# Recurrent mixer: two of four convolution channel groups as 64x64 diagonal products on the array's quarters, and the inversion's small products in turn over the quarters

## Chip, cores and metric

The kernel runs on 1 core of one Trainium2 chip. The metric is the device time of one execution in microseconds (us), the median of several runs.

## What is computed

A trunk of 256 tokens by 1024 features: feed-forward, mixer, feed-forward in each of two layers, with RMS norms around every part. The change is in the first layer's mixer, which has two halves with 512 channels each, a recurrence over 8 heads of 64 and a causal convolution over 31 tokens for each channel by itself:

```python
def mixer_ab(h, ...):
    proj = h @ w_in
    ...
    y = rwkv7_scan(rh, hs(decay), kh, vh, kk, hs(a))
    ...
    y_a = ((y + bonus.reshape(b, t, D_RWKV)) * g.astype(f32)).astype(h.dtype)
    c_val, c_gate = split_cols(proj[..., COLS_RWKV:], [D_CONV, D_CONV])
    glu = c_val * jax.nn.sigmoid(c_gate)
    conv = lax.conv_general_dilated(
        glu, conv_w[:, None, :], window_strides=(1,), padding=[(CONV_WIDTH - 1, 0)],
        dimension_numbers=('NWC', 'WIO', 'NWC'), feature_group_count=D_CONV) + conv_b
    y_b = jax.nn.silu(layer_norm(conv, conv_ln_g, conv_ln_b, CONV_LN_EPS))
    return jnp.concatenate([y_a, y_b], axis=-1) @ w_out
```

The reference runs the recurrence token by token; the kernel runs it in four chunks of 64 tokens, with the inverse of a unit triangular 64x64 matrix for each chunk and head.

## The kernel before

The stages of the program are feed-forward 0, the recurrent mixer (`mixer_a`), feed-forwards 1 and 3, the attention mixer and feed-forward 4. The mixer treated here lies at about 200 to 402 us. Its parts are given out in the order of the table `ORDER`; a scheduler then sets the order on each engine, and every engine works through its own list in order. Products with float32 operands show as two records each in the trace.

The parts that matter, in the order of the program:

- `qmats` and `amats`: products of 64 rows of the chunks, into banks named `acc00` to `acc11`, which `abank` gives out in turn. VectorE evicts those of `amats` (names `ak`, `ar`, lines 816 and 819) with masks.
- `glu`: the input projection of the convolution, gated. It comes in two halves of two channel groups each: `z` (line 843) from PSUM on VectorE, its sigmoid on ScalarE (844), `glu` on VectorE (845).
- `invert`: the blocks of 16 on VectorE, over DRAM; then `doubling`: ten calls of `each`, 16 products of 64x64x64 each, `acc<-T,Q`, `acc<-G,WT`, `acc<-WT,G` (line 585 is the helper that records every small product). The numbers #1 to #10 below are these calls. In `each` all eight heads of one column half come first, then those of the other.
- `bonus`: on GpSimd (POOL), `Wg` and `gg`, lines 884 to 887; `wlo` on line 99 is the lower part of a weight page, some of which POOL makes.
- `conv`: 31 taps (shifts by d tokens) for each of four groups of 128 channels. VectorE has groups 0 and 1 (`feed`, line 924, 60 taps). Group 3 is scaled on ScalarE into `cz` (912) and added on POOL (913). Group 2 is split: 24 taps on TensorE (`pfeed`), each a product with a 128x128 matrix `dw` that holds the tap's weights on its diagonal and is made on ScalarE from the identity (904); the other taps on ScalarE and POOL in a sum of their own. `feed` and `pfeed` say how many taps go behind which instruction.
- `convend` and `conv_norm`: the sums added (961), then transposes (936), statistics, transposes back (949), and the two parts of the output for the projection.
- `state`: for each of four chunks `vz,ak` and `ur` products into `py`, its copy `R` (ScalarE, 982), `pz` = `acc<-R,G`, `vz` (VectorE, 986), `pn` = `acc<-vz,kb`, `SB` (996), `py` again (`gu<-vz,ar`), and at the end of a tile of 128 tokens a norm and transposes (1015).
- `outproj` (370): 96 products of 128x128x512, first those with the convolution's half; then feed-forward 1 begins (223).

Of the kernel before, what the change touches and what calls it, by code (L numbers as in the profile page):

```python
# [39 lines left out]
def label(key):  # L40
    """The kind of a key of weights."""
    if key[0] in "gd":
        return f"{key[0]}{key[2]}" if key[2] < 2 else key[0]
    return "".join(str(z) for z in key)


class Stream:
    """Weights in the order of their use: raw tiles of [128, 1024], and their two parts in pages of float32r."""
# [6 lines left out]
    def add(self, key, ap, cols):  # L55
        """ap: [128, n * 1024] of DRAM; the pages are seen as [128, 1024 // cols, cols]."""
# [36 lines left out]
class Kernel:  # L93
# [21 lines left out]
    def post(self, t, acc, gpost, half, eps, last=False):  # L115
        """x[t] += half * rms_norm(acc) * gpost, the sums in PSUM; eps: of half ** -2 times the mean square."""
# [33 lines left out]
    def pre(self, t, j):  # L150
        """x[t] transposed, times the norm's gains, in two parts; and rstd."""
# [3 lines left out]
        for h in range(2):  # L155
# [3 lines left out]
            for k in range(4):  # L159
                kk = 4 * h + k  # L160
                g = self.gain(j, kk)
                nc.scalar.activation(self.xth[:, kk, ts], ps[:, k * P:(k + 1) * P], AF.Copy, scale=g)  # L162
                nc.vector.scalar_tensor_tensor(out=self.xl(kk)[:, ts], in0=ps[:, k * P:(k + 1) * P], scalar=g,  # L163
                                               in1=self.xth[:, kk, ts].bitcast(F32), op0=ALU.mult, op1=ALU.subtract)
# [11 lines left out]
    def xl_tile(self, h):  # L176
        return self.c.tile([P, 4, 256], F32R, name=f"xl{h}")

# [15 lines left out]
    def units(self):  # L194
        """The parts of a layer's work: ("t", b, t), a block of 256 columns for 128 tokens, or ("c", b, h), 128 columns for all."""
# [7 lines left out]
    def ffn(self, j, rstd, nxt, then):  # L203
        """x += 0.5 * rms_norm(swiglu(rms_norm(x))); then: keys of weights to prepare near the end.
        The factor rstd of the products with w_up is left to the norm behind."""
# [7 lines left out]
        def gu(u):  # L213
            W.upto(self.gkey(j, u))
            G = W.get(self.gkey(j, u))
            if u[0] == "t":
                ps = self.bank("gu", 2)
                n = 0
                for k in range(8):
                    hi, lo = G[k // 2]  # L220
                    xh, xl = (z[:, u[2] * P:(u[2] + 1) * P] for z in (self.xth[:, k, :], self.xl(k)))
# [102 lines left out]
    def abank(self):  # L324
        self.turn = (self.turn + 1) % 4
        return self.bank(("acc00", "acc01", "acc10", "acc11")[self.turn])

    def xunit(self, key, t, late=False):
        """x[t] times a block of 512 columns: [128 tokens, 512] in PSUM; late: not ahead of the latest transposes of x."""
# [3 lines left out]
        for k in range(8):  # L333
            hi, lo = G[k // 2]
            xh, xl = (z[:, t * P:(t + 1) * P] for z in (self.xth[:, k, :], self.xl(k)))
# [6 lines left out]
    def wunit(self, key, groups):  # L342
        """Groups of 128 columns of a block, transposed: [128 columns, group, 256 tokens] in PSUM."""
        ps = self.bank("gu", 2)
        G = self.w.get(key)
        for j, g in enumerate(groups):
            n = 0
            for k in range(8):
                hi, lo = (z[:, k, :] for z in G[g])
                xh, xl = self.xth[:, k, :], self.xl(k)  # L350
# [5 lines left out]
    def outproj(self, j, key, y, nxt, behind=None):  # L356
        """x += rms_norm(y @ w); y(k, t): the two parts of a [128, 128] block of y transposed."""
# [19 lines left out]
    def across(self, rstd):  # L377
        """rstd of the tokens along the free dim, on all partitions: [128, 256]."""
# [10 lines left out]
    def mixer_c(self, j, rstd, nxt, then):  # L389
# [43 lines left out]
        def forget():  # L433
            ps = self.bank("tr", 2)[0:16, 0:256]
            n = 0
            for k in range(8):
                for l, r in ((fhi, self.xth[:, k, :]), (flo, self.xth[:, k, :]), (fhi, self.xl(k))):
# [63 lines left out]
        def values(c, g):  # L501
# [10 lines left out]
            hi, lo = (z[:, g, :] for z in y0) if c == 0 else (self.xth[:, 4 + g, :], self.xl(4 + g))  # L512
# [45 lines left out]
        def y(k, t):  # L558
            ts = slice(t * P, (t + 1) * P)
            return tuple(z[:, ts] for z in ([z[:, k, :] for z in y0] if k < 4 else (self.xth[:, k, :], self.xl(k))))  # L560
# [3 lines left out]
    def mixer_a(self, j, rstd, nxt, then):  # L564
# [9 lines left out]
        # pages of two groups, [2 groups, 2 tiles, 4 * 64]: for both chunks of a tile what pairs with Z (b or u) and what pairs  # L574
        # with V (k or r), on the sides where the state has them
# [6 lines left out]
        m = {}  # L582

# [46 lines left out]
        def shifted(dst, ps, mu, i0):  # L630
            """Token shift of two groups of columns: (1 - mu) * p + mu * p_prev."""
# [7 lines left out]
        def lora():  # L639
# [6 lines left out]
            for dst, b, bias in ((sg, 0, "db"), (ic, 64, "ib")):  # L646
                for h in range(2):
                    ps = self.abank()
# [547 lines left out]
```

## Time and profile before

| what | value |
|---|---|
| median of 3 runs | 1130.53 us (1130.3 to 1131.13) |
| profiled execution, first to last instruction | 1130.1 us |
| TensorE (PE) busy | 1076.5 us, 95% |
| VectorE (DVE) | 669.1 us, 59% |
| ScalarE (ACT) | 568.3 us, 50% |
| GpSimd (POOL) | 256.1 us, 23% |
| mean granted clock of TensorE | 0.981 |
| mixer, the stretch from 300 to 402.5 us | see the rows below |

The profile gives the span of its execution and no other time for it; the median of the runs is 0.4 us above that span. Times in rows count from the start of the span. A row of the timeline merges equal instructions: start, length, engine, line, operation, what is written and read, shapes, their number, and in brackets how long the engine was idle just before and who ended that. For products the shape is rows * columns of the array and then partitions x elements of what is moved.

### The profile page before, as it was taken

To read this page: it belongs to the slowest core of one execution; us is meant where nothing else is said; L and a number is where in the kernel's file an instruction comes from. 1 tells how busy PE (TensorE), PEld (TensorE's weight loads), DVE (VectorE), ACT (ScalarE), POOL (GpSimd) and SP (SyncE) were. 2 spreads that over 40 slices of the span, in tenths; PEclk is the share of its full clock that TensorE was granted. 3 is DMA by queue.
4 is the path that set the end of the run, shared out by engine and by line. 5 is a ranking of instruction groups with operands and counts; after the bars stand their busy time and mean duration, and the time that the engine had idled before them with its cause. 6 is when DMAs were issued, how large, how long until landed. Compare 5 with 4: busy or idle time off the path is not lost.

```text
span 1130.1 us, 17646 instructions
## 1 busy us (share of the span) xinstructions
PE 1076.5 (95%) x6955; PEld 947.5 (84%) x6955; DVE 669.1 (59%) x1064; ACT 568.3 (50%) x933; POOL 256.1 (23%) x194
## 2 busy tenths in 40 slices
PE   7999999978788899999989999999999989999997
PEld 5899988867777789999878999988887768999986
DVE  4465662389888547556535555836667655555722
ACT  7444553554364365345455444635666845444611
POOL 4200006282744051000070000000564541000000
PEclk9999999989988999999999999999999999999999
DMA  9766785154601146557654465744273562665400
GB/s 352 253 209 187 229 305 177 50 166 115 169 2 38 32 174 206 204 187 270 213 176 126 150 244 179 240 157 132 93 284 109 189 202 95 223 189 185 150 1 37
DMA packets 65261, 189.27 MB, mean 167 GB/s; under 512 B 18300, under 2 KB 19612, under 8 KB 65178
## 3 DMA queue, kind: packets, MB, share of 16 engines
q1 hardware_dynamic: 55674, 186.70, 49.2%
q10 hardware_dynamic: 9504, 1.44, 0.7%
q8 instruction: 54, 0.88, 0.3%
q14 instruction: 29, 0.24, 0.1%
HBM read 184.68 MB, written 2.92 MB: 166 GB/s over the span
## 4 chain that ended last, share of the span: by engine, by line
PE 82%; DVE 8%; DMA 3%; ACT 2%; issue 2%; POOL 2%; SPq 0%; POOLq 0%; ACTq 0%; DVEq 0%
PE gu L352 30%; PE acc L263 21%; PE gu L223 15%; PE gu L338 5%; PE acc L370 3%; PE acc L585 2%; PE gu L585 2%; DVE cv L924 2%; DVE wlo L99 2%; DVE x L148 1%; DMA prev<-pv 1%; PE tr L158 1%; POOL p L484 1%; PE tr L243 1%; DMA raw<-in_wgt_dram 1%
## 5 line engine op out<-in xcount | busy, mean ns | idle before, releaser
L98 ACT CAST whi<-raw 128x1024 fp32r<-128x1024 f32 x294 | 303.4, 1048 | 203.7 <-PE gu L352 97.7
L99 DVE TENSOR_TENSOR wlo<-raw,whi 128x1024 fp32r<-128x1024 f32 x248 | 312.2, 1265 | 131.6 <-ACT whi L98 108.6
L352 PE MATMUL gu<-xth,wlo 128*128 128x256 f32 x1104 | 315.0, 285 | 0.0
L352 PE MATMUL gu<-xth,whi 128*128 128x256 f32 x1104 | 314.0, 284 | 0.0
L352 PE MATMUL gu<-xl,whi 128*128 128x256 f32 x1104 | 314.0, 284 | 0.0
L352 PEld LDWEIGHTS gu<-xth,whi 128*128 128x128 f32 x1104 | 212.8, 193 | 3.6 <-issue 1.1
L352 PEld LDWEIGHTS gu<-xth,wlo 128*128 128x128 f32 x1104 | 212.9, 193 | 3.4 <-issue 0.9
L352 PEld LDWEIGHTS gu<-xl,whi 128*128 128x128 f32 x1104 | 212.9, 193 | 1.0 <-issue 0.8
L99 POOL TENSOR_TENSOR wlo<-raw,whi 128x1024 fp32r<-128x1024 f32 x46 | 113.6, 2500 | 300.5 <-PE gu L223 141.8
L263 PE MATMUL acc<-whi,ht 128*128 128x512 f32 x576 | 168.0, 393 | 0.0
L113 POOL TENSOR_TENSOR misc<-misc 128x1 f32<-128x1 f32 (+1 forms) x36 | 31.6, 879 | 475.6 <-DVE misc L130 381.1
L263 PEld LDWEIGHTS acc<-whi,ht 128*128 128x128 f32 x576 | 104.0, 189 | 18.3
L263 PE MATMUL acc<-wlo,ht 128*128 128x512 f32 x288 | 89.9, 392 | 0.0
L234 DVE TENSOR_TENSOR h<-gu,h 128x256 f32<-128x256 f32 x88 | 36.9, 419 | 78.7 <-ACT h L230 75.5
L232 DVE TENSOR_TENSOR h<-gu,misc 128x256 f32<-128x256 f32 x56 | 23.7, 424 | 80.2 <-PE gu L352 80.2
L223 PE MATMUL gu<-whi,xth 128*128 128x512 f32 x160 | 63.7, 402 | 2.4 <-ACT whi L98 2.3
L223 PE MATMUL gu<-wlo,xth 128*128 128x512 f32 x160 | 63.8, 399 | 0.5 <-DVE wlo L99 0.5
L263 PEld LDWEIGHTS acc<-wlo,ht 128*128 128x128 f32 x288 | 53.9, 188 | 11.8
L223 PE MATMUL gu<-whi,xl 128*128 128x512 f32 x160 | 63.2, 399 | 0.4 <-DVE xl L163 0.3
L233 ACT ACTIVATE h<-h 128x256 f32<-128x256 f32 x56 | 23.2, 415 | 54.2 <-DVE h L232 54.2
L230 ACT ACTIVATE h<-gu,misc 128x256 f32<-128x256 f32 x32 | 15.1, 475 | 67.0 <-PE gu L223 37.0
L338 PE MATMUL gu<-whi,xth 128*128 128x512 f32 x112 | 44.8, 400 | 0.5 <-ACT xth L162 0.5
(254 smaller groups left out, 1588.7 us busy)
## 6 DMA issues: line engine op xcount, KB each, us to landing
raw<-in_wgc_dram SPq DMA_DIRECT2D x112, 512.0 KB, 4.5
raw<-in_wd_dram SPq DMA_DIRECT2D x88, 512.0 KB, 4.8
raw<-in_wgt_dram SPq DMA_DIRECT2D x64, 512.0 KB, 5.0
raw<-in_cin_dram SPq DMA_DIRECT2D x24, 512.0 KB, 4.7
raw<-in_ain_dram SPq DMA_DIRECT2D x18, 512.0 KB, 5.3
raw<-in_aout_dram SPq DMA_DIRECT2D x8, 512.0 KB, 5.2
raw<-in_cgate_dram SPq DMA_DIRECT2D x8, 512.0 KB, 10.1
raw<-in_cout_dram SPq DMA_DIRECT2D x8, 512.0 KB, 3.7
```

Source lines behind the costliest of these rows:

```text
L98: self.nc.scalar.copy(out=hi, in_=raw)
L99: (engine or self.nc.vector).tensor_tensor(out=lo, in0=raw, in1=hi.bitcast(F32), op=ALU.subtract)
L113: self.pow = self.nc.gpsimd.tensor_tensor(out=out, in0=v, in1=self.mhalf[:, :n], op=ALU.pow)
L223: nc.tensor.matmul(ps, lhsT=l, rhs=r[:, k % 2], start=n == 0, stop=n == 23)
L232: nc.vector.tensor_tensor(out=z, in0=ps[:, 0:256], in1=self.rb, op=ALU.mult)
L233: nc.scalar.activation(sl, z, AF.Silu)
L234: nc.vector.tensor_tensor(out=h, in0=ps[:, 256:512], in1=sl, op=ALU.mult)
L263: mm = nc.tensor.matmul(out, lhsT=l, rhs=r, start=u[1] == 0 and i + n == 0, stop=u[1] == NB - 1 and i * 3 + n == 5)
L338: self.nc.tensor.matmul(ps, lhsT=l, rhs=r[:, k % 2], start=n == 0, stop=n == 23)
L352: self.nc.tensor.matmul(ps[:, j * 256:(j + 1) * 256], lhsT=l, rhs=r, start=n == 0, stop=n == 23)
L370: self.nc.tensor.matmul(accs[t][c], lhsT=l, rhs=r[:, 0, c * 512:(c + 1) * 512], start=k == ks[0] and n == 0, stop=k == ks[7] and n == 2)
L585: return nc.tensor.matmul(out, lhsT=lhsT, rhs=rhs, start=start, stop=stop, skip_group_check=True)
```

## The change

Group 1 and all of group 2 move to TensorE: all 31 taps, both groups, as four products of 64x64 per tap. Group 1 goes from rows 0-63 to columns 0-63 and from rows 64-127 to columns 64-127 (the bank `gu`); group 2 crosses over, rows 0-63 to columns 64-127 and the other way (the bank `acc11`, which `abank` leaves out meanwhile). The four products of a tap use the four quarters of the array. The host swaps the halves of group 2 in the parameters behind. VectorE keeps group 0, group 3 stays on ScalarE and POOL. The diagonals are now made on POOL, a page of eight taps at a time in two instructions (line 927), from a 128x64 double identity (922). The bias comes in on ScalarE when the two banks are evicted (977). In `qmats`, `amats` and `each` the loops are turned so that successive products alternate between quarters. Line numbers move by a few: 585 becomes 590, 913 becomes 910, 924 becomes 936.

```diff
-CSPLIT, PTAPS = 6, 24
-FEED, PFEED = (4, 3, 12), (1, 2)
+FEED, PFEED = (3, 2, 6), (1, 2)
...
             def each(t, lhsT, rhs):
-                ps = self.abank().rearrange("p (h x) -> p h x", x=64)
-                for c in range(2):
-                    for h in range(8):
+                ps = abank().rearrange("p (h x) -> p h x", x=64)
+                for h in range(8):
+                    for c in range(2):
...
             for d in range(31):
-                for g in range(4):
+                for g in (0, 3):
...
-            m["pconv"] = self.bank("gu", 2)[:, 0:256]
+            m["taps"], m["ptaps"] = iter(taps), iter(range(31))
+            m["busy"] = True
+            m["pconv"] = [self.bank("gu", 2)[:, 0:256], self.bank("acc11")[:, 0:256]]
+
+        def diagonals(q):
+
+            with self.tc.issue_after(m["rkk"].ins):
+                if "e64" not in m:
+                    m["e64"] = self.temp("e64", [64])
+                    nc.gpsimd.tensor_tensor(out=m["e64"], in0=self.ident[:, 0:64], in1=self.ident[:, 64:P], op=ALU.add)
+                n = min(8, 31 - 8 * q)
+                dw = self.page("dw").rearrange("p (g a b) -> p g a b", g=2, b=64)
+                for i in range(2):
+                    o = PAR["cw"] + (1 + i) * 31 + 31 - 8 * q - n
+                    nc.gpsimd.tensor_tensor(out=dw[:, i, 0:n], in0=m["e64"].unsqueeze(1).broadcast_to([P, n, 64]),
+                                            in1=self.sp[:, o:o + n].unsqueeze(2).broadcast_to([P, n, 64]), op=ALU.mult)
+                return dw[:, :, 0:n]
...
-                for d, w in itertools.islice(m.get("ptaps", iter(())), n):
-                    mm(m["pconv"][:, d:256], w, m["glu"][:, 2, 0:256 - d], d == 31 - CSPLIT - PTAPS, d == 30 - CSPLIT)
+                for d in itertools.islice(m.get("ptaps", iter(())), n):
+                    if d % 8 == 0:
+                        m["dw"] = diagonals(d // 8)
+                    j = m["dw"].shape[2] - 1 - d % 8
+                    for i, hp in ((0, 0), (0, 1), (1, 0), (1, 1)):
+                        b, o = 64 * hp, 64 * (hp ^ i)
+                        mm(m["pconv"][i][o:o + 64, d:256], m["dw"][b:b + 64, i, j, :], m["glu"][b:b + 64, 1 + i, 0:256 - d], d == 0, d == 30)
...
-            for d, z in ((31 - CSPLIT - PTAPS, m["pconv"]), (31 - CSPLIT, m["part"])):
-                o = m["cv"][:, 2, d:256]
-                V.tensor_tensor(out=o, in0=z[:, d:256], in1=o, op=ALU.add)
+            for i in range(2):
+                nc.scalar.activation(m["cv"][:, 1 + i, :], m["pconv"][i], AF.Identity, bias=par("cb", 1 + i))
+            m["busy"] = False
```

Three places show how the scheduler's order moves. "waits" lists the engines or DMA queues whose semaphores an instruction waits for.

First, POOL at the group 3 additions. Before, the last additions with the separate sum of group 2 (`cz<-cz`):

```order
L913 TENSOR_TENSOR cv<-cz,cv 128x239 [waits Activation_49,Pool_49]
L913 TENSOR_TENSOR cv<-cz,cv 128x238 [waits Activation_49,Pool_49]
...
L913 TENSOR_TENSOR cz<-cz 128x226 [waits Activation_49,Pool_49]
L913 TENSOR_TENSOR cv<-cz,cv 128x226 [waits Activation_49,Pool_49]
L113 TENSOR_TENSOR misc<-misc 128x1 [waits DVE_49]
```

With the change, additions (910), diagonals (927) and one page of weights (98):

```order
L910 TENSOR_TENSOR cv<-cz,cv 128x240 [waits Activation_49,Pool_49]
L927 TENSOR_TENSOR dw<-e_3005,cst 128x512 [waits PE_49]
L927 TENSOR_TENSOR dw<-e_3005,cst 128x512
L910 TENSOR_TENSOR cv<-cz,cv 128x239 [waits Activation_49,Pool_49]
...
L910 TENSOR_TENSOR cv<-cz,cv 128x226 [waits Activation_49,Pool_49]
L927 TENSOR_TENSOR dw<-e_3005,cst 128x512 [waits PE_49]
L927 TENSOR_TENSOR dw<-e_3005,cst 128x512
L98 TENSOR_TENSOR wlo<-raw,whi 128x1024 [waits DMAHW2_49,DMAHW5_49,DMAHW1_49,DMAHW7_49,DMAHW0_49,PE_49]
L927 TENSOR_TENSOR dw<-e_3005,cst 128x448 [waits DVE_49,PE_49,Pool_49]
L927 TENSOR_TENSOR dw<-e_3005,cst 128x448
```

The diagonals of taps 8 to 15 now stand behind 16 of the 30 additions, those of taps 16 to 23 behind all 30, and those of taps 24 to 30 behind a page of weights as well.

Second, TensorE at the end of the doubling. Before (`T,Q` is #8, `G,WT` are #9 and #10, `glu,dw` taps, `R,G` the first chunk's `pz`):

```order
L585 MATMUL acc_3283<-T,Q 64x64 [waits DVE_49,PE_49]
L585 MATMUL acc_3283<-T,Q 64x64 x15
L585 MATMUL gu<-glu,dw 128x237 [waits Activation_49]
...
L585 MATMUL acc_3334<-G,WT 64x64 x15
L585 MATMUL gu<-glu,dw 128x233 [waits Activation_49]
L585 MATMUL gu<-glu,dw 128x232 [waits Activation_49]
L585 MATMUL acc_3439<-R,G 64x64 [waits DVE_49,Activation_49]
```

With the change (`acc_2980` is the bank of group 2):

```order
L590 MATMUL acc_3291<-T,Q 64x64 x3
L590 MATMUL gu<-glu,dw 64x240 [waits Pool_49]
...
L590 MATMUL acc_3291<-T,Q 64x64 x3
L590 MATMUL acc_2980<-glu,dw 64x240 [waits Pool_49]
...
L590 MATMUL acc_3343<-G,WT 64x64 x15
...
L590 MATMUL gu<-glu,dw 64x232 [waits Pool_49]
...
L590 MATMUL acc_2980<-glu,dw 64x232 [waits Pool_49]
...
L953 MATMUL tr<-cst,cv 128x128 [waits Activation_49]
...
L590 MATMUL acc_3485<-R,G 64x64 x8
```

The taps stand behind the doubling as before, but they wait for POOL instead of ScalarE, the second page's waits lie inside #8, and the last seven taps are 28 products in a row (14 for one bank, then 14 for the other) ahead of the first `pz`.

Third, VectorE at the second half of `glu`. Before:

```order
L845 TENSOR_TENSOR glu<-cv,z 128x512 [waits DMAHW3_49,DMAHW2_49,Activation_49]
L816 TENSOR_TENSOR ak<-acc_3033,cst 64x4x64 [waits PE_49]
...
L924 SCALAR_TENSOR_TENSOR cv<-glu,cst,cv 128x254 [waits DVE_49] x2
L843 TENSOR_TENSOR z<-gu,misc 128x512 [waits Pool_49]
L816 TENSOR_TENSOR ak<-acc_3053,cst 64x4x64 [waits PE_49]
```

With the change:

```order
L850 TENSOR_TENSOR glu<-cv,z 128x512 [waits PE_49,Activation_49]
L848 TENSOR_TENSOR z<-gu,misc 128x512 [waits PE_49,Pool_49]
L821 TENSOR_TENSOR ak<-acc_2995,cst 64x4x64 [waits PE_49]
...
L824 TENSOR_TENSOR ar<-acc_3021,cst 128x4x64
L850 TENSOR_TENSOR glu<-cv,z 128x512 [waits Activation_49]
L936 SCALAR_TENSOR_TENSOR cv<-glu,cst,cv 128x254 [waits DVE_49]
```

The second `z` moves from behind four taps and six evictions to right behind the first `glu`, with its wait for POOL.

## Rows read from the trace of the kernel before

**Rows 1.** The page, part 4: the chain that ended last, by engine.

```profile
PE 82%; DVE 8%; DMA 3%; ACT 2%; issue 2%; POOL 2%; SPq 0%; POOLq 0%; ACTq 0%; DVEq 0%
```

**Rows 2.** Windows: start:end, us, busy of PE, PEld, DVE, ACT, POOL, PEclk, DMA, GB/s.

```profile
300.00:313.40 13.40, 3.01 (x34) 2.80 (x33) 13.25 (x21) 6.14 (x16) 8.82 (x4) 0.74 0.55 136
...
346.80:357.70 10.90, 8.24 (x78) 6.81 (x77) 10.80 (x22) 2.79 (x6) 3.86 (x6) 0.69 0.00 0
```

**Rows 3.** Timeline of ScalarE.

```profile
310.27 6.23 ACT L904 ACTIVATE dw<-cst 128x128 f32<-128x128 f32 x21
...
335.68 0.58 ACT L982 COPY R<-gu 64x512 f32<-64x512 f32 x1 [6.39 <-PE gu L585]
```

**Rows 4.** Timeline of TensorE, first taps and start of the doubling.

```profile
313.37 3.55 PE L585 MATMUL gu<-glu,dw 128*128 128x255 f32 x8 [9.42 <-ACT dw L904]
...
319.43 1.11 PE L585 MATMUL gu<-glu,dw 128*128 128x251 f32 x4
...
320.48 1.90 PE L585 MATMUL acc<-T,Q 64*64 64x64 f32 x32
```

**Rows 5.** Timeline of VectorE, from the first evictions to the second glu.

```profile
300.16 0.41 DVE L816 TENSOR_TENSOR ak<-acc,cst 64x256 f32<-64x256 f32 x1
...
304.96 4.14 DVE L924 SCALAR_TENSOR_TENSOR cv<-glu,cst,cv 128x254 f32<-128x254 f32 x2
...
312.53 0.69 DVE L845 TENSOR_TENSOR glu<-cv,z 128x512 f32<-128x512 f32 x1
```

**Rows 6.** Timeline of GpSimd.

```profile
278.60 3.86 POOL L791 TENSOR_TENSOR sq<-r,k 128x1024 f32<-128x1024 f32 x1 [19.70 <-DVE r L637]
...
286.96 2.22 POOL L884 TENSOR_TENSOR Wg<-pv,misc 128x512 f32<-128x512 f32 x2 [4.50 <-DVE misc L798]
...
289.14 3.42 POOL L885 TENSOR_TENSOR Wg<-Wg,ln 128x512 f32<-128x512 f32 x2
...
303.83 4.99 POOL L99 TENSOR_TENSOR wlo<-raw,whi 128x1024 fp32r<-128x1024 f32 x2
...
318.83 12.37 POOL L913 TENSOR_TENSOR cv<-cz,cv 128x255 f32<-128x255 f32 x16 [10.01 <-ACT cz L912]
```

**Rows 7.** Timeline of TensorE, products on parts of the array.

```profile
264.59 2.35 PE L585 MATMUL acc<-ur,bk 64*64 64x64 f32 x64 [0.28 <-DVE bk L691]
...
360.79 0.69 PE L585 MATMUL acc<-vz,kb 128*64 128x64 f32 x16
...
363.82 0.65 PE L585 MATMUL acc<-SB,cst 64*64 64x256 f32 x4
```

**Rows 8.** Timeline of TensorE, from the first chunk's pz to feed-forward 1.

```profile
346.84 1.14 PE L585 MATMUL acc<-R,G 64*64 64x64 f32 x16
...
352.04 1.12 PE L585 MATMUL acc<-vz,kb 128*64 128x64 f32 x16 [2.66 <-DVE vz L986]
...
358.33 1.14 PE L585 MATMUL acc<-R,G 64*64 64x64 f32 x16
...
366.52 1.14 PE L585 MATMUL acc<-R,G 64*64 64x64 f32 x16 [0.18 <-ACT R L982]
...
382.75 0.73 PE L370 MATMUL acc<-whi,xth 128*128 128x512 f32 x2
...
388.33 0.39 PE L370 MATMUL acc<-whi,xth 128*128 128x512 f32 x1
...
393.84 0.63 PE L158 MATMUL tr<-cst,x 128*128 128x128 f32 x4 [2.19 <-DVE x L148]
...
402.52 0.39 PE L223 MATMUL gu<-whi,xl 128*128 128x512 f32 x1
```

**Rows 9.** Windows of 1 us, PE alone: start:end, us, busy, PEclk, DMA, GB/s.

```profile
306.00:307.00 1.00, 0.00 (x0) 0.69 1.01 276
...
316.00:317.00 1.00, 1.00 (x5) 0.69 0.00 0
...
357.00:358.00 1.00, 1.00 (x6) 0.71 0.00 0
```

More of the change, by code (lines that the diff above doesn't have):

```diff
@@ L177, in xl_tile, with xh @@
         return self.c.tile([P, 4, 256], F32R, name=f"xl{h}")
+    def xh(self, k):
+        return self.xth[k // 4][:, k % 4, :]
     def xl(self, k):
@@ L220, in gu @@
                     hi, lo = G[k // 2]
-                    xh, xl = (z[:, u[2] * P:(u[2] + 1) * P] for z in (self.xth[:, k, :], self.xl(k)))
+                    xh, xl = (z[:, u[2] * P:(u[2] + 1) * P] for z in (self.xh(k), self.xl(k)))
                     for l, r in self.passes(xh, xl, hi, lo):
@@ L322, in small, with abank @@
         return self.misc[:, o:o + n]
-    def abank(self):
-        self.turn = (self.turn + 1) % 4
+    def abank(self, n=4):
+        self.turn = (self.turn + 1) % n
         return self.bank(("acc00", "acc01", "acc10", "acc11")[self.turn])
@@ L334, in xunit @@
             hi, lo = G[k // 2]
-            xh, xl = (z[:, t * P:(t + 1) * P] for z in (self.xth[:, k, :], self.xl(k)))
+            xh, xl = (z[:, t * P:(t + 1) * P] for z in (self.xh(k), self.xl(k)))
             with self.tc.issue_after(self.turned.ins) if late else contextlib.nullcontext():
@@ L559, in y @@
             ts = slice(t * P, (t + 1) * P)
-            return tuple(z[:, ts] for z in ([z[:, k, :] for z in y0] if k < 4 else (self.xth[:, k, :], self.xl(k))))
+            return tuple(z[:, ts] for z in ([z[:, k, :] for z in y0] if k < 4 else (self.xh(k), self.xl(k))))
         return self.outproj(j, "co", y, nxt)
@@ L582, in mixer_a, with abank @@
         m = {}
+        def abank():
+            return self.abank(3 if m.get("busy") else 4)
         def mm(out, lhsT, rhs, start=True, stop=True):
@@ L719, in qmats @@
             for t in range(2):
-                pss = [self.abank()[:, 0:256].rearrange("p (g x) -> p g x", x=64) for _ in range(2)]
-                for hp in range(2):
+                pss = [abank()[:, 0:256].rearrange("p (g x) -> p g x", x=64) for _ in range(2)]
+                for g in range(4):
                     for c in range(2):
-                        for g in range(4):
+                        for hp in range(2):
                             b, o = 64 * hp, 64 * (c ^ hp)
@@ L790, in receptance @@
             rk = m["sq"]
-            nc.gpsimd.tensor_tensor(out=rk, in0=r, in1=k, op=ALU.mult)
+            m["rkk"] = nc.gpsimd.tensor_tensor(out=rk, in0=r, in1=k, op=ALU.mult)
             psb = self.bank("tr", 2)
@@ L806, in amats @@
                 t, c = ch // 2, ch % 2
-                pss = [self.abank().rearrange("p (g x) -> p g x", x=P) for _ in range(2)]
+                pss = [abank().rearrange("p (g x) -> p g x", x=P) for _ in range(2)]
                 cs = slice(64 * c, 64 * c + 64)
-                for hp in range(2):
-                    for g in range(4):
+                for g in range(4):
+                    for hp in range(2):
                         b = slice(64 * hp, 64 * hp + 64)
@@ L891, in conv @@
             scratch = grp(self.temp("cz", [1024]))
-            part = m["part"] = scratch[:, 3, :]
-            turn, taps, ptaps = 0, [], []
+            turn, taps = 0, []
             for d in range(31):
-                for g in range(4):
+                for g in (0, 3):
                     w = par("cw", g * 31 + 30 - d)
@@ L898, in conv @@
                         nc.scalar.activation(cv[:, g, :], gl[:, g, :], AF.Identity, scale=w, bias=par("cb", g))
-                    elif g == 2 and 31 - CSPLIT - PTAPS <= d < 31 - CSPLIT:
-                        i = len(ptaps)
-                        if i % 8 == 0:
-                            dw = grp128(self.page("dw"))
-                        with self.tc.issue_after(m["gate"].ins):
-                            nc.scalar.activation(dw[:, i % 8, :], self.ident, AF.Copy, scale=w)
-                        ptaps.append((d, dw[:, i % 8, :]))
-                    elif g == 2 and d == 31 - CSPLIT:
-                        nc.scalar.activation(part[:, d:256], gl[:, g, 0:256 - d], AF.Copy, scale=w)
-                    elif g == 3 or g == 2 and d > 31 - CSPLIT:
+                    elif g == 3:
                         z = scratch[:, turn % 3, 0:256 - d]
                         turn += 1
-                        o = cv[:, g, d:256] if g == 3 else part[:, d:256]
+                        o = cv[:, g, d:256]
                         nc.scalar.activation(z, gl[:, g, 0:256 - d], AF.Copy, scale=w)
@@ L1025, in mixer_a @@
             W.upto(key)
-        return self.outproj(j, "ao", lambda k, t: tuple(z[:, t * P:(t + 1) * P] for z in (self.xth[:, k, :], self.xl(k))), nxt, m["last"])
+        return self.outproj(j, "ao", lambda k, t: tuple(z[:, t * P:(t + 1) * P] for z in (self.xh(k), self.xl(k))), nxt, m["last"])
     def par(self, name, i=0):
@@ L1100, in run @@
             nc.sync.dma_start(out=cst[:, 384:896], in_=a["cst"][:, 384:896])
-            self.xth = c.tile([P, 8, 256], F32R, name="xth")
+            self.xth = [c.tile([P, 4, 256], F32R, name=f"xh{h}") for h in range(2)]
             self.c = c
```

30 lines of the change are left out of this document (15 added, 15 removed).

## The prediction

> **What bounds the kernel now.** I read the page first: the chain that ended last runs through TensorE for 82% of the span [rows 1], so outside the mixer there is nothing for this change to win. Inside the mixer I read the timeline of each engine between 264 and 403 us and the windows. Two stretches stand out: 300 to 313.4, where TensorE works for 3.0 of 13.4 us, and 346.8 to 357.7, 8.2 of 10.9 at a mean granted clock of 0.69 [rows 2]. In the first, TensorE stands 9.42 us before its first tap, until ScalarE has made a diagonal [rows 4], and ScalarE makes them only behind the second `glu` [rows 3, 5]. In the second it stands 2.66 us for `vz` [rows 8], which on VectorE lies behind taps. Both idle times are followed by TensorE's lower level, 1.2 GHz: the granted clock falls from 1.00 to 0.50 in the window 306-307 and comes back in 316-317, some 3 us after work returned at 313.4; after the 2.66 us it comes back in 357-358, some 5 us after 352 [rows 9, 8]. Any new wait of over 2 us must therefore be expected to cost slow work behind it.
>
> **The start moves forward.** The second `z` waits for POOL's last `gg` product. Before, that ends where the pair of `wlo` begins, 303.83, with one more `wlo` ahead of it (4.99 for two, so 2.5 each [rows 6]); now that page stands behind, so `z` can start at 301.3, takes some 0.7 (as `glu`) with 0.7 for the sigmoid hidden, and six evictions of 0.41 and one tap, at the slow 2.07 that taps take beside POOL's `wlo`, stand between it and `glu` [rows 5]: 301.3 + 0.7 + 2.5 + 2.1 + 0.7 = 307.3, against 313.2 before. The evictions of the first chunk wait 1.6 longer for that; only `amats` of later chunks stands behind them, and it needs `glu` anyway by its taps. TensorE then needed 4.2 us from 313.37 to the start of the doubling, which is the first row of #2 less its 2.87 period, 320.48 - 2.87 = 317.6 [rows 4]; I add 0.5 for the two chunks of `amats` that now stand between the taps. The doubling starts at 312.0 instead of 317.6. That is 5.6 us, and the question is how much of it survives.
>
> **POOL becomes the pacemaker.** Its first three new instructions (double identity, page 1) fit into the idle 4.50 before `Wg` [rows 6]: a 128x512 product cost 1.11 there, at worst 1.71 as the next pair, so 2.5 to 3.9 in all. The group 3 additions therefore begin behind the `wlo` pair, at 308.8, not at 318.83. Each takes 0.773 (12.37 for 16 [rows 6]). So: 16 additions to 321.2; page 2, two products of 1.11, usable half by half at 322.3 and 323.4; 14 additions to 334.2; page 3 at 335.3 and 336.4; then one `wlo` of 2.5, and page 4. On SP a load whose page POOL must free first now stands ahead of the loads of the second tile's inverse; POOL frees it between the pair that ends at 292.6 and the `wlo` pair at 303.8 [rows 6], and the loads are due at 312, so it costs nothing unless POOL falls 8 us behind. ScalarE is not the limit: it loses 24 diagonals (6.23 for 21 [rows 3]) and the scalings of group 2.
>
> **TensorE under that pace.** A call of `each` took 1.83 for 32 records, 58 ns apart, all in one quarter after another. `qmats`, whose records change quarter more often, took 2.35 for 64, 37 ns each [rows 7]: 1.2 for a call now, bounds 1.0 and 1.83. A tap is four products, eight records of 256 columns. The nearest row is `acc<-SB,cst`, two products on two diagonal quarters, both into one bank: four records in 0.65, where four full-array records took 1.11 [rows 4, 7]; two at a time, then, some 0.21 to 0.26 per pair. No row has all four quarters busy. `acc<-vz,kb`, two column halves in turn, ran 16 records in 0.69 [rows 7], so columns overlap as well as rows, and I take rows and columns together: 0.45 per tap, with 0.9 (two at a time) as the upper bound. A call with its two taps is 2.1 instead of 2.87.
>
> #1 and #2 end at 316.2, #3 with 0.3 for `WT` at 317.7. Taps 8 and 9 wait for page 2 until 322.3: 4.6 us of idle. The low clock follows, so the taps and #4 take double: 327.6. #5, #6, #7 and the start of #8 bring 334.2; page 3 comes at 335.3; taps 16 and 17 end at 336.9, #8 at 337.8, its next taps at 338.7, #9 with 0.8 for `WT` at 341.6, #10 at 342.8 (343.7 with its taps). Page 4 waits for #10 and for the `wlo` that started behind #8 (337.8 + 2.5): halves at 343.9 and 345.0. The last seven taps use only two quarters at a time, bank by bank: 7 x 0.43 twice, 346.9 and 349.9. ScalarE's eviction of the bank frees `acc11`, and the first `pz` starts at 350.5 against 346.84 [rows 8]: **3.7 us later**, though the doubling began 5.6 earlier. Bounds: +0.7 (pages at 0.7 each, four quarters throughout) and +10 (below).
>
> **Behind the first `pz` it gains.** Before, 55.7 us pass from there to feed-forward 1, 346.84 to 402.52. Four things change, all from [rows 8]. The convolution is complete, so no taps stand ahead of `vz`, the 2.66 idle and its low clock go, and the first interval of 11.5 (346.84 to 358.33) becomes like the second, 8.2: -3.3. The convolution's part of the projection is ready a chunk earlier, so twelve products at 0.2325 (24 between 382.75 and 388.33) that ran behind the fourth chunk fit into earlier waits: -2.8. The end keeps a wait for the last transposes, but 1.3 instead of 2.19, and without low clock behind it: -0.9 and about -0.9. On the other side the transposes of the next stage's input, which before began at 393.84 ahead of the last projection products, now all follow them: +1.4 for the first evictions, and +0.5 for two products of feed-forward 1 that ran early. Together -6.0, with bounds -3 (the first interval alone) and -9. The 60 taps of VectorE becoming 30 costs and gives nothing more: no wait of TensorE is left on them. The eviction with the bias takes the place of two additions on VectorE: nothing.
>
> **Sum**, against the profiled span: 1130.1 + 3.7 - 6.0 = 1127.8; the median lies 0.4 above the span, so **1128.2 us**. A measurement of this kernel tells 0.2%, 2.3 us, from no change; the forecast is at its edge.
>
> **Rivals.** *Two quarters at a time* (15%). If rows and columns don't overlap at once, a tap is 0.9: up to #8 POOL's pages hide that, behind it eight taps add 3.4. 1131.6, no change. For it: no row shows four quarters at work; against: only that rows overlap in one row of the trace and columns in another.
>
> *Banks in turn* (6%). Each bank receives products of both row halves, in the taps and in `each`. If those have to take turns, the last seven taps double, +5.9, the eight ahead of them +3.4, and `each` stays at 1.83, +1.7 for the part behind page 3: 1139. Against it stands `acc<-SB,cst`, both row halves into one bank in 0.65 [rows 7], which is shorter than even four full records one after another. This is what the Trainium skill's page "TensorEngine Tiling (Array Packing)", section "Gotcha 1: PSUM Pressure", would have: it says that different row tiles cannot use the same PSUM bank simultaneously. By that sentence the change would lose some 9 us; the row disagrees, and I follow the row.
>
> *POOL later still* (19%), the case on the other side. One mechanism: the diagonals' pages stand behind the additions on one in-order engine, and both run slow beside VectorE, as the pair of 3.42 beside 2.22 shows. At 1.71 a page's product, the four on the path add 2.4; at 0.83 an addition, 30 add 1.7; and a 2 us wait for page 3 brings the low clock for #8 to #10, 3 us. First `pz` at 357.6, 1135. From a first `pz` at 352.8 on nothing is won, from 355 on it is slower.
>
> *POOL quicker* (15%). If pages cost 0.7 and the restart keeps its clock, the first `pz` stands at 347.5 and the rest gains 9 at best: 1122. This needs page 2 before 321.
>
> That the change does nothing, because POOL holds TensorE to the old pace, is the forecast's own middle, not a case apart.
>
> **How the numbers follow.** Forecast 45%; its own range of -6 to +2 us is 1124.5 to 1132.5, about half of it faster than 1128.2, nearly half within 2.3 us. With 15% for the quicker POOL: faster 0.42; the middle of the forecast and two quarters at a time: 0.30; slower: 0.28, from the late POOL, the banks and the tails. The range takes in both POOL cases and leaves out the banks and the far ends: 1120.5 to 1136.
>
> **What would show it.** Right: the first group 3 addition near 309 and a period of 0.75 to 0.8; the wait before tap 8 ends on POOL near 322; taps' records start four at a time; the first `pz` near 350, the second 8 us behind it, feed-forward 1 from about 400. Wrong: a first `pz` past 355 or before 348, a first interval that stays near 11, records of a tap that start in pairs (two quarters) or `each` still at 1.83 (banks).

## The result: 1.4% slower, and the profile after

The change takes 1146.9 us (median of 4 runs, 1146.1 to 1149.1) against 1130.4: a ratio of 1.0141, with an interval of 1.0126 to 1.0155. I had predicted 1128.2, and 1136 as the end of the range. The profiled span is 1144.7 us, the mean granted clock 0.974 against 0.981. The page's chain by engine is below. It is followed back only to 279.5 us, so its shares add up to 76%, and TensorE's 63% can't be set against the 82% of [rows 1], nor GpSimd's 3% against 2%:

```profile
PE 63%; DVE 6%; POOL 3%; ACT 2%; issue 1%; DMA 1%; ACTq 0%; POOLq 0%; DVEq 0%
```

The timeline of TensorE from the start of the doubling to the second `pz`, the stretch of [rows 4, 8]:

```profile
317.86 1.04 PE L590 MATMUL acc<-T,Q 64*64 64x64 f32 x30
318.68 0.43 PE L590 MATMUL acc<-glu,dw 64*64 64x252 f32 x2
...
321.20 0.38 PE L590 MATMUL gu<-glu,dw 64*64 64x249 f32 x2
337.92 1.86 PE L590 MATMUL acc<-G,WT 64*64 64x64 f32 x30 [16.34 <-DVE WT L869]
...
355.22 1.09 PE L590 MATMUL acc<-G,WT 64*64 64x64 f32 x30 [3.18 <-DVE WT L869]
...
359.24 2.35 PE L590 MATMUL gu<-glu,dw 64*64 64x232 f32 x22
361.88 2.29 PE L590 MATMUL acc<-glu,dw 64*64 64x231 f32 x22
...
366.01 1.14 PE L590 MATMUL acc<-R,G 64*64 64x64 f32 x16
...
373.64 1.14 PE L590 MATMUL acc<-R,G 64*64 64x64 f32 x16
```

The products are as quick as forecast: a call of `each` lasts 1.04 us where it took 1.90 [rows 4], and two taps of two groups fit into the 1 us behind it. But ahead of #3 the array stands for 16.34 us, where I had 0.3. What ended it stands on two other engines. VectorE around the second `glu` and the first `WT`:

```profile
300.35 0.62 DVE L776 COPY inv<-inv 128x256 f32<-128x256 f32 x1
...
309.41 1.95 DVE L850 TENSOR_TENSOR glu<-cv,z 128x512 f32<-128x512 f32 x1
...
337.17 0.69 DVE L869 TENSOR_TENSOR WT<-acc,cst 128x512 f32<-128x512 f32 x1 [14.54 <-POOL cv L910]
```

GpSimd in the same stretch, the counterpart of [rows 6]:

```profile
312.47 12.87 POOL L910 TENSOR_TENSOR cv<-cz,cv 128x255 f32<-128x255 f32 x16 [1.66 <-ACT cz L909]
325.29 2.05 POOL L927 TENSOR_TENSOR dw<-e,cst 128x512 f32<-128x512 f32 x2
327.30 9.84 POOL L910 TENSOR_TENSOR cv<-cz,cv 128x239 f32<-128x239 f32 x14
...
358.24 1.83 POOL L927 TENSOR_TENSOR dw<-e,cst 128x448 f32<-128x448 f32 x2 [4.42 <-PE acc L590]
```

The array's first `WT` product needs VectorE's `WT`, and VectorE waits 14.54 us for GpSimd's additions of group 3: they end at 327.30 + 9.84 = 337.14, `WT` starts at 337.17. `WT` uses no result of them. In the changed program the page of `WT` lies where `cz`, the scratch of group 3, lay (the two have the same place in SBUF), and whoever writes it first must wait until the last of the 30 additions has read `cz`.

In the kernel before, `WT` shared a page too, with the diagonals of the first eight taps. TensorE's last taps on these, and VectorE's first `WT` there:

```profile
322.30 1.11 PE L585 MATMUL gu<-glu,dw 128*128 128x249 f32 x4
```

```profile
323.44 1.29 DVE L864 TENSOR_TENSOR WT<-acc,cst 128x512 f32<-128x512 f32 x2 [4.44 <-PE gu L585]
```

It waited 4.44 us for taps whose sum it does not read; the eighth ends at 322.30 + 1.11 = 323.41. The array lost only 0.78 us by that, ahead of #3 at 324.19.

The windows show what the clock does in the change meanwhile (start:end, us, PE busy, PEclk, DMA, GB/s). It falls from 1.00 to 0.50 in the wait, and #3 then takes 1.86 us where #1 took 1.04:

```profile
304.00:308.00 4.00, 3.50 (x18) 0.50 0.67 149
...
312.00:316.00 4.00, 4.00 (x22) 0.50 0.01 4
316.00:320.00 4.00, 4.00 (x85) 0.96 0.34 87
320.00:324.00 4.00, 1.58 (x42) 1.00 0.13 48
324.00:328.00 4.00, 0.00 (x0) 0.82 0.00 0
...
336.00:340.00 4.00, 2.08 (x38) 0.50 0.00 0
340.00:344.00 4.00, 4.00 (x64) 0.55 0.00 0
```

### The profile page after: what moved, and what is told of

It reads as the page before. It is cut to its first block, busy times and chain, and to the rows that moved or that the text cites. A ratio compares the mean times of both kernels' runs of the same rounds, so it can differ in the third digit from the quotient of the medians.

```text
span 1144.7 us, 17976 instructions
## 1 busy us (share of the span) xinstructions
PE 1079.5 (94%) x7155; PEld 948.3 (83%) x7155; DVE 660.4 (58%) x1032; ACT 558.3 (49%) x903; POOL 262.7 (23%) x198
## 4 chain that ended last, share of the span: by engine, by line
PE 63%; DVE 6%; POOL 3%; ACT 2%; issue 1%; DMA 1%; ACTq 0%; POOLq 0%; DVEq 0%
PE gu L354 23%; PE acc L265 16%; PE gu L225 11%; PE gu L340 4%; PE acc L372 3%; POOL cv L910 2%; PE acc L590 1%; DVE x L147 1%; PE gu L590 1%; DVE cv L936 1%; DVE tmp L771 1%; DVE wlo L98 1%; PE tr L157 1%; POOL p L486 1%; PE tr L508 0%
## 5 line engine op out<-in xcount | busy, mean ns | idle before, releaser
L354 PE MATMUL gu<-xh,wlo 128*128 128x256 f32 x1104 | 316.1, 286 | 0.0
L354 PE MATMUL gu<-xh,whi 128*128 128x256 f32 x1104 | 314.8, 285 | 0.0
L354 PEld LDWEIGHTS gu<-xh,wlo 128*128 128x128 f32 x1104 | 213.7, 194 | 3.4 <-issue 0.9
L354 PEld LDWEIGHTS gu<-xh,whi 128*128 128x128 f32 x1104 | 213.6, 193 | 3.5 <-issue 1.1
L225 PE MATMUL gu<-whi,xh 128*128 128x512 f32 x160 | 63.7, 402 | 3.3 <-ACT whi L97 2.3
L225 PE MATMUL gu<-wlo,xh 128*128 128x512 f32 x160 | 63.8, 399 | 0.5 <-DVE wlo L98 0.5
L97 ACT CAST fhi<-raw 128x1024 fp32r<-128x1024 f32 x40 | 41.6, 1046 | 17.1 <-DMA raw<-in_wgt_dram 13.5
L340 PE MATMUL gu<-whi,xh 128*128 128x512 f32 x112 | 45.3, 405 | 2.2 <-ACT v L425 1.8
```

The lines of the kernel that those rows point to most:

```text
L97: self.nc.scalar.copy(out=hi, in_=raw)
L225: nc.tensor.matmul(ps, lhsT=l, rhs=r[:, k % 2], start=n == 0, stop=n == 23)
L340: self.nc.tensor.matmul(ps, lhsT=l, rhs=r[:, k % 2], start=n == 0, stop=n == 23)
L354: self.nc.tensor.matmul(ps[:, j * 256:(j + 1) * 256], lhsT=l, rhs=r, start=n == 0, stop=n == 23)
```

## The experiments

Theory A was the shared page; theory B, its rival, GpSimd's pace with the pages of diagonals. They are told apart by taking away one, the other, and both. All ratios below are to the kernel before, run on the same chip.

**Own pages for `WT`**, and for the second `ar`, in two pages whose content is dead by then:

```diff
-            inv = self.page("inv")
+            inv = m["inv"] = self.page("inv")
-            ar = m["ar"] = [self.page("ar")... for _ in range(2)]
+            ar = m["ar"] = [z... for z in (self.page("ar"), m["sq"]...)]
-            WT = blk(self.c.tile([P, 1024], F32, name="WT", tag="xl0"))
+            WT = blk(m["inv"])
```

> The change with the doubling's scratch WT laid in the page of inv (dead since G's transposes went out) and the second ar page in the page of sq (dead since the bonus): no page of the doubling is shared with the third group's scratch cz any more. Theory A (the shared page: WT waits for the last of the 30 additions of group 3, so #3 starts at 337.9): the 16.3 us gap before #3 goes. What is late next is page 2 of the diagonals, which here stands behind 20 additions (20 x 0.8 from 312.5, and 2.1: ready near 331), so taps 8 and 9 wait until then: 7 to 10 us less, 1137 to 1140 us. Theory B (not the shared page but GpSimd's pace holds the stage, its pages of diagonals being due): 1145 to 1149, the gap only changes its name.

Measured: 1150.2 us, ratio 1.0169 (1.0148 to 1.019). Both ranges were missed, B's by 1.2 us. TensorE no longer waits for `WT` (the name is `inv` now), only to stand for the next page:

```profile
326.12 1.09 PE L590 MATMUL acc<-G,inv 64*64 64x64 f32 x32
...
336.41 1.50 PE L590 MATMUL gu<-glu,dw 64*64 64x248 f32 x6 [8.74 <-POOL dw L927]
```

GpSimd says why that page is late, and ScalarE why GpSimd is:

```profile
320.11 15.25 POOL L910 TENSOR_TENSOR cv<-cz,cv 128x255 f32<-128x255 f32 x20 [13.41 <-ACT cz L909]
335.31 2.04 POOL L927 TENSOR_TENSOR dw<-e,cst 128x512 f32<-128x512 f32 x2
```

```profile
319.52 1.30 ACT L909 ACTIVATE cz<-glu,cst 128x255 f32<-128x255 f32 x3 [11.64 <-PE acc L590]
```

With two pages taken out, the others were laid anew: `cz` now lies on a page that the array reads until the last chunk of `amats`, so the additions start 8 us later than in the change, and page 2 stands behind 20 of them. The shared page was moved, not removed.

**No later pages**, with `WT` shared and with its own page: `if d % 8 == 0` becomes `if d == 0`, which leaves out pages 2 to 4, so all 31 taps use page 1.

> The change with page 1 of the diagonals used for all 31 taps: pages 2 to 4 are not made (taps 8 to 30 have the wrong weights). WT still shares its page with cz. Theory A: the doubling still stands until the last addition, which ends 1 to 3 us earlier as page 2 isn't made between the additions; the waits for page 4 at the tail go too (up to 4 us): 1140 to 1145. Theory B: without the pages the stage is free: 1130 to 1136.

> Both at once: WT and the second ar page in dead pages, and page 1 of the diagonals for all taps (taps 8 to 30 have the wrong weights). Theory A: neither the shared page nor later pages hold the array; the doubling runs through from 318 with 10 products of 1.2 us and 20 taps of 0.5, first pz near 344: 1124 to 1129. Theory B: as with the one page alone, within 2 us of it.

Measured: 1142.1 (ratio 1.0092, 1.0072 to 1.0112) with the shared page, 1134.7 (1.0031, 1.0018 to 1.0043) without. Theory A's size for the first holds, and B falls as the only cause: leaving out the pages alone gives 4.8 us, where B had 11 or more. TensorE with the shared page:

```profile
335.49 1.87 PE L590 MATMUL acc<-G,WT 64*64 64x64 f32 x30 [9.46 <-DVE WT L869]
```

and with its own:

```profile
326.40 1.04 PE L590 MATMUL acc<-G,inv 64*64 64x64 f32 x30
```

The 9.46 us are gone, and 7.5 of them arrive in the time. So the shared page is shown as the wait before #3; but 1134.7 is outside A's 1124 to 1129, so something else is late too: the doubling starts at 321.1 here, not at 318, nor at the 312 of the prediction.

The four times belong together: 1146.9 for the change, 1150.2 with `WT` on its own page, 1142.1 without later pages, 1134.7 with both. Each edit alone gives +3.3 and -4.8 us, the two together -12.2: where one wait goes, the other still stands. So the pages of diagonals are a second cause beside the shared page. How much of the 15.5 us between 1150.2 and 1134.7 is their making, and how much the additions' start (320.1 against 311.7), these runs do not separate.

**The turned loops alone, and everything but them:** the order of the loops in `qmats`, `amats` and `each`, put into the kernel before and taken out of the change.

> The kernel before with nothing but the turned loops: the small products of qmats, amats and each go round the quarters, the convolution stays as it was. My prediction's price: each call 1.90 to 1.2 us, so 10 calls give 7 us to the stretch of the doubling, but the group-3 additions of GpSimd, the taps of 1.4 us and the end of the convolution stay: 1124 to 1130. Rival (the products of different quarters can't be written to one bank at a time, so the turn gains nothing): 1130 to 1132.

> The change without its turned loops: qmats, amats and each run quarter by quarter as before, the taps stay on the quarters. WT still shares the page of cz. Theory A (shared page and the waits behind it hold the stage): the wait before #3 ends at the same addition, near 338; of the 0.8 us more per call only what lies behind it counts, eight calls, less what the waits for pages 3 and 4 hide: 2 to 6 us more than the change, 1149 to 1153. Rival (the turn gains nothing beside the taps): 1146 to 1148.

Measured: on the kernel before, 1126.9, ratio 0.9957 (0.9945 to 0.997), inside my range: this version beats both. Taken out of the change, 1146.4, ratio 1.0147 (1.0106 to 1.0187), the same as with them: theory A's 1149 to 1153 was missed, the rival's range held. I take it that in the change the array waits for GpSimd, be the calls quick or slow; this is not shown, since the profiled run was the slowest of the four, at 1153.6. TensorE of the loops alone:

```profile
322.01 1.15 PE L585 MATMUL acc<-T,Q 64*64 64x64 f32 x32
...
338.50 1.87 PE L585 MATMUL acc<-T,Q 64*64 64x64 f32 x32 [2.98 <-DVE T L872]
...
351.09 0.69 PE L585 MATMUL acc<-vz,kb 128*64 128x64 f32 x16 [1.28 <-DVE vz L986]
```

A call costs 1.15 instead of 1.90 [rows 4], but the first `pz` still starts at 347.3 (346.84 before): at 338.5 the array waits for VectorE, which has nine taps ahead of the sum. What is won comes behind `pz`, 777.4 us to the end of the span instead of 783.3; the wait for `vz` has halved [rows 8]. Fewer taps there, `FEED` (4, 3, 8), change nothing:

> The kernel before with the turned loops, and 8 instead of 12 taps fed to VectorE behind each sum of the doubling. In the run of the turned loops alone the array stands 3.0 us at 335.5 for VectorE's sums behind nine taps. If those taps set the pace of the quicker calls, the four taps held back fall behind the doubling, where VectorE has room between the chunks of the state: 1124 to 1126. Rival: they only move to the wait for vz behind the first pz: 1126 to 1129.

Measured: 1127.6, 0.9965 (0.9952 to 0.9978): the rival.

**The order on GpSimd**, with own pages: the last 20 additions are given out behind pages 2 and 3.

```diff
+                        if d in (8, 16):
+                            m["thirds"](10 if d == 8 else 99, m["dwi"])
```

> Own pages as in the first run, and the order on GpSimd set: 10 additions of group 3, page 2 of the diagonals, 10 additions, page 3, the last 10 (before: 20, page 2, 10, page 3). Computes the same. Theory A2 (what own pages gained at #3 it lost again behind page 2, which came at 337.3 behind 20 additions): page 2 comes 10 x 0.76 = 7.6 us earlier, near 329.7; the doubling waits 2 to 3 us before taps 8 and 9 instead of 8.7, and page 3 no longer ends anything: 7 to 10 us less than own pages, 1140 to 1143; if the first addition starts near 312 again and not at 320, 1135 to 1138. Theory B (the order of GpSimd is no matter, own pages lost by the later start alone): 1147 to 1151.

Measured: 1143.6, 1.0111 (1.0091 to 1.0131), 6.6 us less than own pages and 0.6 above theory A2's range; its mechanism is right:

```profile
320.44 7.90 POOL L917 TENSOR_TENSOR cv<-cz,cv 128x255 f32<-128x255 f32 x10 [13.40 <-ACT cz L916]
328.30 2.04 POOL L934 TENSOR_TENSOR dw<-e,cst 128x512 f32<-128x512 f32 x2
...
351.84 1.82 POOL L934 TENSOR_TENSOR dw<-e,cst 128x448 f32<-128x448 f32 x2
```

Page 2 comes 7 us earlier; now page 4 is awaited for 3.36 at 352.8, and the additions still start at 320.

**Page 1 ahead of the inversion.** My second theory, C: page 1 on GpSimd, new in the change, pushes the bonus onto the inversion, whose copy ends at 301.0 instead of 296.1. One edit, `issue_after` the inversion's copy instead of the bonus' product, led the scheduler to make page 1 at 5.5 us. It was run without later pages, on the change itself, and with the set order:

> Own pages and one page of diagonals (taps 8 to 30 with the wrong weights), and that page is made ahead of the inversion, before the bonus, instead of between the two. Theory C (page 1 on GpSimd pushes the bonus onto the inversion, and the two engines slow each other; this makes the second glu and so the doubling late): the inversion's copy is done near 295 as in the kernel before, the doubling starts 3 to 5 us earlier, 316 to 318: 1129 to 1132. Rival D (the start is set by amats on the array at its lower clock, 3.1 us a chunk, whatever the inversion does): start at 320 to 321, 1133 to 1136.

> The change with nothing but page 1 of the diagonals made ahead of the inversion; WT still shares its page with cz, so #3 still waits for the last addition of group 3. Theory C (page 1 between the product for the bonus and the bonus pushes the bonus onto the inversion; that made the second glu late): inversion's copy done near 297.5 instead of 301, second glu 4 to 5 us earlier, the additions and with them the end of the wait before #3 3 to 4 us earlier: 1142 to 1145. Rival (the wait before #3 is held by something else than the additions' end): 1146 to 1148.

> All three at once, and it computes the same: own pages, 10 additions ahead of each page on GpSimd, page 1 ahead of the inversion. If the parts add up (1143.6 for the first two, 3.6 us for page 1 as in the runs without later pages): 1139 to 1141. If the additions still start only at 320, since cz stands in a page that the array reads until amats ends, the earlier glu gives little: 1142 to 1144.

Measured: 1131.1 (ratio 0.9997, 0.9984 to 1.001), 3.6 less than own_no_pages and in C's range, though the doubling starts only 1.3 us earlier, at 319.8, where C had 316 to 318; but on the change 1159.2 (1.0245, 1.0225 to 1.0265), 12 more; and with the set order 1144.5 (1.0116), no gain and 0.5 above the higher of its two ranges. VectorE of page1_early:

```profile
289.86 0.41 DVE L752 TENSOR_TENSOR inv<-inv,c 128x256 f32<-128x256 f32 x1
...
304.17 0.38 DVE L776 COPY inv<-inv 128x256 f32<-128x256 f32 x1
...
344.69 0.69 DVE L869 TENSOR_TENSOR WT<-acc,cst 128x512 f32<-128x512 f32 x1 [16.04 <-POOL cv L910]
```

The inversion starts at 289.9 instead of 283.7; from 270 us to its start VectorE has seven splits of weights instead of three. And in own_pages, with page 1 where the change has it, the copy ended at 296.8. So C falls as a rule. I take it that the inversion is late by which splits the scheduler puts around its steps and by what GpSimd does beside them, and that page 1 is only one of the things that shift this; no run tests that alone. `WT` waits 16.0 here too: the shared page again.

**Taps of TensorE.** Two more suspects for what is left: seven taps between the doubling and the first `pz` (4.9 us from 359.24 on in the change), and the taps between the chunks of `amats`. `PFEED` becomes (1, 3), then (0, 3), without later pages:

> Own pages, page 1 alone and early (taps 8 to 30 with the wrong weights), and three taps instead of two on TensorE behind each call of the doubling, so that all 31 are through before it ends. Theory E (what is left of the loss is seven taps behind the doubling, 3.7 us between its last call and the first pz, which the kernel before had on VectorE): first pz 2 to 4 us earlier, 1127 to 1129. Rival (the taps only move, the array is the limit of the doubling): 1130 to 1132.

> Own pages, page 1 alone and early (taps 8 to 30 with the wrong weights), no taps between the chunks of amats, three behind each call of the doubling. Theory F (what still makes the doubling start at 320 is that chunks of amats stand behind taps, which wait for glu, and then run 3.1 us each at 1.2 GHz): the chunks run ahead of the second glu, the doubling starts 4 to 8 us earlier, 312 to 316: 1122 to 1127. Rival G (the array's lower clock stays whatever stands between, since it idled before; or the evictions of amats stand behind glu on VectorE anyway): start at 317 to 320, 1127 to 1131.

Measured: 1129.5 (0.9975, 0.9965 to 0.9986) and 1127.8 (0.9971, 0.9961 to 0.9981). Of E little is left: 1.6 us, 0.5 above its range, and the first `pz` stays at 350, since the doubling now ends later by what the tail saves. Of F the mechanism is shown, and the doubling starts earlier than F had it; the time is in the range of its rival G. TensorE of early_amats_clear:

```profile
307.37 2.04 PE L590 MATMUL acc<-ur,bk 64*128 64x128 f32 x8 [5.17 <-DVE ar L824]
309.34 1.86 PE L590 MATMUL acc<-T,Q 64*64 64x64 f32 x30
...
323.09 1.09 PE L590 MATMUL acc<-G,inv 64*64 64x64 f32 x30 [2.05 <-DVE inv L869]
```

The doubling starts at 309.3 instead of 320.1, yet `pz` only at 346.6 instead of 350.1. VectorE holds the rest:

```profile
307.47 0.47 DVE L936 SCALAR_TENSOR_TENSOR cv<-glu,cst,cv 128x255 f32<-128x255 f32 x1
...
316.31 6.13 DVE L936 SCALAR_TENSOR_TENSOR cv<-glu,cst,cv 128x249 f32<-128x249 f32 x6
322.36 0.68 DVE L869 TENSOR_TENSOR inv<-acc,cst 128x512 f32<-128x512 f32 x1
```

GpSimd beside these six taps:

```profile
315.79 2.36 POOL L98 TENSOR_TENSOR wlo<-raw,whi 128x1024 fp32r<-128x1024 f32 x1
318.10 18.67 POOL L910 TENSOR_TENSOR cv<-cz,cv 128x249 f32<-128x249 f32 x24
```

A tap takes 0.47 us alone. Six of them stand ahead of the second `WT` (named `inv` here), for which the array waits 2.05 us: the first takes 2.11, beside GpSimd's split of a weight page, the other five 0.72 to 0.81, beside its additions.

The same two edits with all pages made (own pages and set order), and a late first tap on the turned loops alone:

> The corrected change of own pages, set order and early page 1, with three taps behind each call. It computes the same. Theory E without a limit from the pages: 2 to 4 us less than with two taps, 1136 to 1140. Rival: pages 2 and 3 come too late for three taps a call and the wait takes the gain: within 1 us of the two-tap version.

> The corrected change (own pages, 10 additions ahead of each page on GpSimd; it computes the same) with no taps between the chunks of amats and three behind each call. In own_order cz stood in a page that the array reads until the last chunk of amats, so the additions began at 320. Theory F: amats ends 4 to 8 us earlier, and with it the additions, pages 2 and 3 and the doubling all come earlier: 1134 to 1140. Rival G: 1141 to 1145.

> The kernel before with the turned loops, taps only behind the last chunk of amats (two) and three behind each call of the doubling instead of two. Theory F: the other chunks no longer wait for the diagonals behind the second glu, the doubling starts 2 to 5 us earlier than 318.5 and all 24 taps are through before it ends: 1121 to 1125. Rival G: no change against the turned loops alone, 1125 to 1129.

Measured: 1142.8 (1.01, 1.0072 to 1.0128), 1141.7 (1.0105, 1.008 to 1.013) and 1135.9 (1.0036, 1.0018 to 1.0054). None is in the range of its theory: the first is 2.8 us above E's and 1.7 from its two-tap version, the second is in G's range, the third above both. In the second and the third, what F moves does come earlier, and the next wait takes it. In own_order_amats_clear the additions start at 307.9, but page 2 gets its page from the array only at 324.2, and page 4 ends a wait of 7.33. GpSimd there:

```profile
307.92 8.24 POOL L917 TENSOR_TENSOR cv<-cz,cv 128x255 f32<-128x255 f32 x10 [1.66 <-DVE ak L821]
324.19 2.05 POOL L934 TENSOR_TENSOR dw<-e,cst 128x512 f32<-128x512 f32 x2 [8.03 <-PE acc L590]
```

In turned_first_tap_late the doubling starts at 314.7 instead of 318.5, as F says, but VectorE has six taps ahead of its first `WT` (320.53, 4.68 us), and the array waits 6.04 for it: the kernel is 11 us above the upper end of F's range.

## Why the prediction was wrong

The step that failed is this one: "#1 and #2 end at 316.2, #3 with 0.3 for `WT` at 317.7." I priced `WT` by its length and the hand-over, and took the waits of the changed program from what each instruction reads. What it writes has a wait too. The trace before shows one, the 4.44 us of `WT` behind the eighth tap, which cost the array little (0.78 us); the prediction does not count it. In the change the last reader of the page is the 30th addition, and the array stands 16.34 us. Against the steps of the prediction, in spans (1144.7 against 1127.8; 317.7 is the end of #3, so its start is 316.5):

| step | predicted | measured | difference |
|---|---|---|---|
| second `glu` done | 307.3 | 311.4 | +4.1 |
| from there to the doubling | 4.7 | 6.5 | +1.8 |
| from the doubling's start to the start of #3 | 4.5 | 20.1 | +15.6 |
| from there to the first `pz` | 34.0 | 28.1 | -5.9 |
| from the first `pz` to the end | 777.3 | 778.7 | +1.4 |

- **Prices of the products: right.** I had 1.2 for a call and 0.45 for a tap; a call takes 1.04, and a tap at full clock 0.48 for its four products in both banks: two of them lie between 318.68, where the first call's products run out, and 319.64, where the next call begins. In the tail, bank by bank, 22 records of the taps' products take 2.35 us at 359.24, some 0.2 for each pair, so the four pairs of a tap would take 0.8 there. The records do start in pairs, which I had named as the sign of two quarters; but the 0.48 shows all four at work, so that rival fell. So did the banks in turn: each pair of the tail is of both row halves and goes to one bank, in 0.2 us, less than one full-array record of a tap takes (1.11 for four [rows 4]). By the Trainium skill, page "TensorEngine Tiling (Array Packing)", section "Gotcha 1: PSUM Pressure", different row tiles can't use one bank simultaneously; the trace disagrees.
- **The start: 5.9 us too early.** I let the inversion stay where it was; its copy ended 4.9 later. And the 0.5 us that I added for `amats` between the taps was too little: the last two chunks, 16 records each, take 3.09 us at 309.49 and 2.18 at 315.27, the granted clock at 0.50 until 316. Taking the taps out from between the chunks brought the start from 320.1 to 309.3. I had also misread the first tap of the kernel before: ScalarE makes diagonals there from 310.27 on [rows 3], so by these rows what the tap waited for until 313.37 was the second `glu`, done at 313.22 [rows 5]. The sum counts from that `glu` and is not touched.
- **The wait before #3: missed.** My 4.6 us for page 2, behind #3, went into it: page 2 was whole at 327.3 where I had 323.4, and the wait ended at 337.9 anyway. "POOL later still" had the sign and the engine, at 1135, but not the mechanism: its price was slow pages, and what counted was the end of all 30 additions.
- **From #3 on: 5.9 us less than I had**, mostly since the 4.6 us of idle for page 2 were not there. Page 3 lies where page 2 lay and waited for the array to read that:

```profile
347.95 2.20 POOL L927 TENSOR_TENSOR dw<-e,cst 128x512 f32<-128x512 f32 x2 [10.82 <-PE acc L590]
```

- **The low clock: not after each such wait.** I expected slow work behind any new wait of over 2 us. Ahead of #9 the array stands 3.18 us, and the granted clock stays at 1.00; #9 takes 1.09 us:

```profile
352.00:356.00 4.00, 0.82 (x28) 1.00 0.68 182
```

- **Behind the first `pz`: nearly right**, a gain of 4.6 against 6.0; the first interval fell from 11.5 [rows 8] to 7.6 us.

Would it have come to 1128 without the shared page? No: with it gone and no later page to make, 1134.7 remain; only with page 1 early, three taps a call and `amats` clear of taps as well does the kernel come to 1127.8, still with page 1 alone. No version that makes all pages of diagonals has a median below 1141. What stays open is a layout that makes all pages and in which `cz`, `WT` and the pages of diagonals share with nobody; none was run.

## What to carry to other kernels

When a change alters which tiles live when, read for each new or moved write who last read its place: a tile that has nothing to do with the work can hold it, and in the trace it shows as a wait on an engine whose result the waiting instruction does not use. Look for such waits in the trace before the change too, also where they cost nothing yet. Moving a tile by hand moved the sharing elsewhere here, so look for the next wait before pricing the gain. Of a change with two parts, measure each alone: here the one that touched nothing but the order of loops gave 0.4% by itself, and with the other it gave nothing.

## What the runs showed of the hardware

- A tap on VectorE, with two inputs in SBUF, takes 0.47 us alone, 0.72 to 0.81 beside GpSimd's additions of 0.78, and 2.11 beside its split of 2.36 (early_amats_clear, above); the eviction into `inv` behind them keeps 0.68. The Trainium skill, page "SBUF — State Buffer", section "SBUF: two separate sides", says that such an instruction and a GpSimd one hold a pair of ports in turn, each for its whole length; the rows agree.
- The array's clock stayed at 1.2 GHz through unbroken work of very different length. In own_pages the array worked without idle from 307.4 on, chunks of `amats`, taps and two calls of the doubling, and the clock rose only in the window 324 to 325; in the change it worked from 304.5 on and the clock rose in 316 to 317; in turned_first_tap_late it worked from 308.0 on and the clock rose in 312 to 313; in the kernel before it worked from 313.4 on, taps on the whole array, and the clock had begun to rise in the window 316 to 317 [rows 9]. Windows of own_pages:

```profile
323.00:324.00 1.00, 1.00 (x16) 0.50 0.00 0
324.00:325.00 1.00, 1.00 (x32) 0.94 0.00 0
```
